# x given channel-major as well: transposes of x replaced, norm statistics by sums over partitions, first half projections on unnormalised x

## The chip, the cores and the metric

One core of one Trainium2 chip runs the kernel. The metric is the device time of one execution in microseconds (us). TensorE is called PE, its weight loads PEld, VectorE DVE, ScalarE ACT, GpSimd POOL and SyncE SP. Here SP issues every DMA; POOL and ACT issue none.

## The reference

```python
h = rmsnorm(x, norm_g)                                  # x: 1 x 2048 x 1024, float32
proj = h @ w_in                                         # 1024 -> 7680
glu_in, conv_gate, q, k, v, attn_gate, merge_logits = split(proj)
c = conformer_conv(glu_in, ...)                         # a*sigmoid(b), 31-tap depthwise conv, layernorm, silu
y_conv = (c * silu(conv_gate)) @ w_conv_out
a = sliding_window_attention(rope(q), rope(k), v, sinks)
y_attn = (a * silu(attn_gate)) @ w_attn_out
g_conv, g_attn = split(sigmoid(merge_logits))
x = x + (g_conv * y_conv + g_attn * y_attn) @ w_out
return rmsnorm(x, final_norm_g)
```

`rmsnorm(x, g)` is `x * rsqrt(mean(x*x over channels) + 1e-5) * g`, one factor for each position and one gain for each channel.

## The kernel before, in words

The 2048 positions go through in two sweeps of 1024 positions, and each sweep in two halves of 512. A projection computes 128 output channels for 512 positions (a half projection): 8 channel blocks k of 128, and for each of them three matmuls, since every float32 operand is held as a high part (rounded) and a low part (the rest): high x high, high x low, low x high. So a half projection is 24 matmuls of 128 x 128 by 128 x 512 into one bank of PSUM. Weights are split by `load_w`: SP loads a raw half (kh, four blocks k, 256 KB), ACT copies it to the high part, POOL subtracts to get the low part (lines 253 and 242), and `keep` stores the low part to DRAM, so that a second load of the same weight takes it from there. Raw, high and low tiles have four buffers each (`stage`), results three PSUM banks (`mm_ps`, tag mm) and three more for transposes, attention and the like (`tp_ps`, tag tp).

PE's right-hand operands are the tiles hT: normalised x, channels on partitions, positions along the row, high and low part, 8 tiles for each half. x comes position-major. For the first sweep `build_h_first` squares and sums each 128 positions on ACT (line 350), takes the root (351), reciprocal (353) and scales (354), and then PE transposes 128 x 128 pieces (line 361), four into one bank; ACT writes the high part times the gain (363), DVE the low part (364). The first half's transposes stand on PE ahead of the first product, the second half's among the first products. For the second sweep `build_h` does this among the output projections of the first sweep (lines 314 to 334; transposes on line 327), one block of 128 positions after another.

The first sweep begins with gb and ga (the two glu projections of channel block 0) and ka (the first of k's two). Of each the first half is computed, then of each the second half, with the weights loaded twice. Then follow kb, v, q, the other glu projections at given places, the four gates, attention and the convolution alongside, layernorm, the projections ya, yc and at last the output projection o (line 885), with the final norm.

PE's instructions run in the order in which the program writes them. On the other engines and in SP's queue a planner orders them ahead of time, by a priority (early in the program is high, evacuations of PSUM are raised by PRIO, chains of the class `Line` by twice that) and by its own estimate of when operands are ready; on the chip each engine then runs its order strictly. `Line` hangs background work (convolution taps, layernorm steps, attention chains) among PE's blocks by an estimated time.

Of the kernel before, what the change touches and what calls it, by code (L numbers as in the profile page):

```python
# [19 lines left out]
P = 128  # L20
# [33 lines left out]
def hybrid_block(ctx: ExitStack, tc: tile.TileContext, x, par_d, w_in, w_conv, sinks, w_attn, w_out,  # L54
# [47 lines left out]
    def load_first(half):  # L102
        xs = []
        for j in range(4):
            r0 = (4 * half + j) * P
            xs.append(slot(A[7 * half + j], [P, D], F32, f"xf{half}_{j}"))
            nc.sync.dma_start(out=xs[-1], in_=x2[r0:r0 + P, :])
        return xs

    x_first = load_first(0)  # L110

# [21 lines left out]
    nc.sync.dma_start(out=sink_bc, in_=sinks.partition_broadcast(P).rearrange("p o h -> p (o h)"))  # L133
    dve.tensor_scalar(out=nsink, in0=sink_bc, scalar1=-1.0, scalar2=None, op0=ALU.mult)
    par = const.tile([P, KC, NR], F32, name="par")
    nc.sync.dma_start(out=par, in_=par_d)
# [107 lines left out]
    def load_w(src, name):  # L244
# [3 lines left out]
        for kh in range(2):  # L248
            raw = stage.tile([P, 4, P], F32, tag="raw", name=f"raw_{name}{kh}")
            nc.sync.dma_start(out=raw, in_=src[:, 4 * kh:4 * kh + 4, :])  # L250
            hi = stage.tile([P, 4, P], F32R, tag="whi", name=f"whi_{name}{kh}")
            lo = stage.tile([P, 4, P], F32R, tag="wlo", name=f"wlo_{name}{kh}")
            act.copy(hi, raw)  # L253
            if (at, kh) in lo_stored:
                nc.sync.dma_start(out=f(lo), in_=d_lo[at, kh])
            else:
                split_lo(lo, raw, hi, pool)
            parts.append((hi, lo))

# [7 lines left out]
    def project(src, rhs, name, evac, halves=(0, 1)):  # L267
# [6 lines left out]
        def blocks():  # L274
            for half in halves:
                ps = mm_ps.tile([P, TH], F32, tag="mm", name=f"mm_{name}{half}")
                for k in range(KC):
                    whi, wlo = got["w"][0](k)
                    r = rhs(k, half)
                    for i, (a, b) in enumerate(((whi, r[:, 0, :]), (whi, r[:, 1, :]), (wlo, r[:, 0, :]))):  # L280
                        pe.matmul(out=ps, lhsT=a, rhs=b, start=(k == 0 and i == 0),  # L281
                                  stop=(k == KC - 1 and i == 2))
# [7 lines left out]
        def by_halves():  # L290
            return [project(src, rhs, f"{name}{h}", evac, (h,)) for h in range(2)]

        return prefetch, blocks, by_halves
# [13 lines left out]
    def build_h(s, b, tiles):  # L307

        r0 = s * T + b * P
        xt, ss = [], work.tile([P, 2], F32, tag="ss", name=f"ss{s}_{b}")  # L310
        for i in range(2):
            xh = raw_tile(f"x{s}_{b}_{i}")
            nc.sync.dma_start(out=xh, in_=x2[r0:r0 + P, i * TH:(i + 1) * TH])
            act.activation(out=t2k(f"sq{s}_{b}_{i}"), in_=xh, func=AF.Square,
                           accum_out=ss[:, i:i + 1])
            xt.append(xh)
        rs = work.tile([P, 2], F32, tag="rs", name=f"rs{s}_{b}")
        dve.tensor_tensor(out=rs[:, 0:1], in0=ss[:, 0:1], in1=ss[:, 1:2], op=ALU.add)
        act.activation(out=rs[:, 1:2], in_=rs[:, 0:1], func=AF.Sqrt, bias=eps, scale=1.0 / D)
        dve.reciprocal(out=rs[:, 0:1], in_=rs[:, 1:2])  # L320
        for i in range(2):
            dve.tensor_scalar(out=xt[i], in0=xt[i], scalar1=rs[:, 0:1], scalar2=None, op0=ALU.mult)
        yield 0.0, 8.0
        for i in range(2):
            tp = tp_ps.tile([P, 4, P], F32, tag="tp", name=f"tpx{s}_{b}_{i}")
            for j in range(4):
                pe.transpose(out=tp[:, j, :], in_=xt[i][:, j * P:(j + 1) * P], identity=ident)
            hs = t2k(f"hs{s}_{b}_{i}").rearrange("p (a b) -> p a b", b=P)
            dve.tensor_tensor(out=hs, in0=tp, in1=g_norm[:, 4 * i:4 * i + 4, :].broadcast_to([P, 4, P]),
                              op=ALU.mult)  # L330
            c0 = (b % 4) * P
            for j in range(4):
                dst = tiles[4 * i + j]
                act.copy(dst[:, 0, c0:c0 + P], hs[:, j, :])
                split_lo(dst[:, 1, c0:c0 + P], hs[:, j, :], dst[:, 0, c0:c0 + P], dve)
            yield 0.44, (1.0 if i == 0 else 0.0)
# [5 lines left out]
    ht = [make_tiles(h_tags[0], 0, "hT0_"), None]  # L342

    def build_h_first(half, xs):

        ss = work.tile([P, 2, 4], F32, tag="ss0", name=f"ssf{half}")
        for j in range(4):
            xt = xs[j]
            sq = slot(C[j], [P, D], F32, f"sqf{half}_{j}")
# [6 lines left out]
        if half == 1:  # L356
            ht[1] = make_tiles(h_tags[0], 1, "hT0_")
        for k in range(KC):
            tp = tp_ps.tile([P, 4, P], F32, tag="tp", name=f"tpf{half}_{k}")
            for j in range(4):  # L360
                pe.transpose(out=tp[:, j, :], in_=xs[j][:, k * P:(k + 1) * P], identity=ident)
# [603 lines left out]
```

## Time and profile before

| | |
|---|---|
| three runs | 2027.36, 2027.73, 2027.74 us; median 2027.73 us |
| profiled execution | 2027.62 us, of which span 2025.9 us |
| PE busy | 2004.9 us (99%) |
| DVE, ACT, POOL busy | 1324.1 (65%), 1026.0 (51%), 403.4 us (20%) |
| DMA queue | 354.16 MB, 53.9% of 16 engines |

Busy times are sums over the instructions of an engine within the span; the execution's own time holds 1.72 us that lie around the span. A group of instructions is named by its line, its engine, what it writes and reads, and its shape.

### The profile page before, as it was taken

To read this page: it belongs to the slowest core of one execution; us is meant where nothing else is said; L and a number is where in the kernel's file an instruction comes from. 1 tells how busy PE (TensorE), PEld (TensorE's weight loads), DVE (VectorE), ACT (ScalarE), POOL (GpSimd) and SP (SyncE) were. 2 spreads that over 40 slices of the span, in tenths; PEclk is the share of its full clock that TensorE was granted. 3 is DMA by queue.
4 is the path that set the end of the run, shared out by engine and by line. 5 is a ranking of instruction groups with operands and counts; after the bars stand their busy time and mean duration, and the time that the engine had idled before them with its cause. 6 is when DMAs were issued, how large, how long until landed. Compare 5 with 4: busy or idle time off the path is not lost.

```text
span 2025.9 us, 27562 instructions
## 1 busy us (share of the span) xinstructions
PE 2004.9 (99%) x9256; PEld 1666.9 (82%) x9256; DVE 1324.1 (65%) x1965; ACT 1026.0 (51%) x2313; POOL 403.4 (20%) x336
## 2 busy tenths in 40 slices
PE   7999999999999999999999999999999999999998
PEld 6888888888888888888888888888888888888887
DVE  4968779988994365123668678699888924431324
ACT  6312577767777463123533225777777764621222
POOL 2335332333323223241001120110111100001200
PEclk9999999999999999999999999999999999999999
DMA  7445655555566757445343556555555577564432
GB/s 252 146 146 167 212 172 159 161 170 180 161 189 213 245 188 249 150 151 178 134 147 132 167 181 196 159 178 177 176 157 174 175 231 260 176 229 140 152 114 83
DMA packets 265821, 355.91 MB, mean 176 GB/s; under 512 B 28112, under 2 KB 126544, under 8 KB 265680
## 3 DMA queue, kind: packets, MB, share of 16 engines
q1 hardware_dynamic: 265680, 354.16, 53.9%
q8 instruction: 73, 1.20, 0.2%
q14 instruction: 68, 0.56, 0.1%
HBM read 234.51 MB, written 119.54 MB: 175 GB/s over the span
## 4 chain that ended last, share of the span: by engine, by line
PE 94%; DVE 4%; DMA 1%; issue 0%; ACT 0%; SPq 0%; POOL 0%; DVEq 0%; ACTq 0%; POOLq 0%
PE mm_ma L281 9%; PE o L885 9%; PE mm_mc L281 9%; PE mm_yc L281 9%; PE mm_ya L281 9%; PE mm_ga L281 9%; PE mm_gb L281 8%; PE mm_cg L281 8%; PE mm_ag L281 6%; PE mm_q_a L281 4%; PE mm_q_b L281 4%; PE sc L572 3%; DVE acc L396 3%; PE ov L622 2%; PE mm_v L281 2%; PE tpp L602 1%
## 5 line engine op out<-in xcount | busy, mean ns | idle before, releaser
L396 DVE SCALAR_TENSOR_TENSOR acc<-glu,par,acc 128x1024 f32<-128x1024 f32 x464 | 595.9, 1284 | 6.2
L885 PE MATMUL o<-wo,mT 128*128 128x512 f32 x768 | 178.3, 391 | 0.0
L885 PEld LDWEIGHTS o<-wo,mT 128*128 128x128 f32 x768 | 143.1, 188 | 29.2
L281 PE MATMUL mm_cg<-hT,whi_cg 128*128 128x512 f32 x512 | 159.6, 393 | 0.0
L281 PE MATMUL mm_ma<-hT,whi_ma 128*128 128x512 f32 x512 | 159.6, 393 | 0.0
L281 PE MATMUL mm_ga<-hT,whi_ga 128*128 128x512 f32 x512 | 159.4, 392 | 0.2 <-ACT whi_ga L253 0.2
L281 PE MATMUL mm_ag<-hT,whi_ag 128*128 128x512 f32 x512 | 159.4, 392 | 0.0
L281 PE MATMUL mm_gb<-hT,whi_gb 128*128 128x512 f32 x512 | 159.2, 392 | 0.0
L281 PE MATMUL mm_mc<-hT,whi_mc 128*128 128x512 f32 x512 | 157.9, 389 | 0.0
L281 PE MATMUL mm_yc<-uT,whi_yc 128*128 128x512 f32 x512 | 157.7, 389 | 0.0
L281 PE MATMUL mm_ya<-aT,whi_ya 128*128 128x512 f32 x512 | 157.7, 389 | 0.0
L613 POOL TENSOR_SCALAR_AFFINE_SELECT pc<-pt 128x1024 fp32r<-128x1024 f32 x60 | 65.7, 1094 | 422.1 <-DVE pt L242 413.4
L281 PEld LDWEIGHTS mm_ya<-aT,whi_ya 128*128 128x128 f32 x512 | 96.1, 188 | 20.1
L281 PEld LDWEIGHTS mm_yc<-uT,whi_yc 128*128 128x128 f32 x512 | 96.1, 188 | 20.0
L281 PEld LDWEIGHTS mm_mc<-hT,whi_mc 128*128 128x128 f32 x512 | 95.9, 188 | 20.0
L281 PEld LDWEIGHTS mm_ga<-hT,whi_ga 128*128 128x128 f32 x512 | 94.4, 188 | 19.1 <-ACT whi_ga L253 0.6
L281 PEld LDWEIGHTS mm_gb<-hT,whi_gb 128*128 128x128 f32 x512 | 94.6, 188 | 18.6
L281 PEld LDWEIGHTS mm_ag<-hT,whi_ag 128*128 128x128 f32 x512 | 94.2, 188 | 18.3
L281 PEld LDWEIGHTS mm_ma<-hT,whi_ma 128*128 128x128 f32 x512 | 94.1, 188 | 18.1
L281 PEld LDWEIGHTS mm_cg<-hT,whi_cg 128*128 128x128 f32 x512 | 94.0, 188 | 18.1
L592 ACT ACTIVATE ss<-ss,st 128x128 f32<-128x128 f32 x256 | 99.7, 390 | 11.2 <-DVE st L587 10.6
L281 PE MATMUL mm_ga<-hT,wlo_ga 128*128 128x512 f32 x256 | 99.9, 390 | 0.7 <-POOL wlo_ga L242 0.7
(364 smaller groups left out, 4244.5 us busy)
## 6 DMA issues: line engine op xcount, KB each, us to landing
qk<-d_q SPq DMA_DIRECT2D x256, 64.0 KB, 2.2
d_a<-ss SPq DMA_DIRECT2D x128, 128.0 KB, 1.9
aT<-d_a SPq DMA_DIRECT2D x32, 512.0 KB, 5.7
qk<-d_k SPq DMA_DIRECT2D x240, 64.0 KB, 2.0
raw_gb<-in_w_in_dram SPq DMA_DIRECT2D x34, 256.0 KB, 3.4
raw_ga<-in_w_in_dram SPq DMA_DIRECT2D x34, 256.0 KB, 3.3
raw_ag<-in_w_in_dram SPq DMA_DIRECT2D x32, 256.0 KB, 3.6
d_ag<-ag SPq DMA_DIRECT2D x32, 256.0 KB, 2.2
```

The lines of the kernel that those rows point to most:

```text
L281: pe.matmul(out=ps, lhsT=a, rhs=b, start=(k == 0 and i == 0), stop=(k == KC - 1 and i == 2))
L396: dve.scalar_tensor_tensor(out=to, in0=glu[c][:, j:j + T], scalar=tap(c, j), in1=acc[c], op0=ALU.mult, op1=ALU.add)
L572: pe.matmul(out=o, lhsT=q[:, h, :], rhs=r, start=(j == 0), stop=(j == 1))
L592: act.activation(out=sb[:, h, :], in_=sb[:, h, :], func=AF.Exp, scale=SCALE, bias=ngm[:, h:h + 1], accum_out=den[:, h:h + 1])
L602: pe.transpose(out=tpp[:, h, :], in_=sb[:, h, :], identity=ident)
L613: pool.affine_select(out=pc, in_=f(pt), pattern=[[0, 2], [0, GQ], [1, P]], compare_op=ALU.is_ge, fill=0.0, base=0, channel_multiplier=-1)
L622: pe.matmul(out=ov, lhsT=vv, rhs=pp[:, i % 2], start=(i == 0), stop=(i == nm - 1))
L885: pe.matmul(out=ps, lhsT=a[:, c0:c0 + P], rhs=r, start=(k == 0 and i == 0), stop=(k == KC - 1 and i == 2))
```

## The change

A second copy of x, `xt`, is given channel-major (8 blocks of 128 channels by 2048 positions). All transposes of x go. Squares are summed over the 8 channel blocks elementwise (`add_square`: ACT squares, DVE or POOL adds), and the sum over the 128 partitions is two matmuls with a constant tile `ones` of 1/1024 (`norm_chain`), whose result has the mean square in every partition; ACT takes the root and DVE two reciprocals of 128 x 256, which gives `rs`, a 128 x 512 tile of factors.

In the first sweep `opening` runs six projections (gb, ga, ka, kb, q0a, q0b) for the first half on `u`, which is x times the gain, split in high and low, not normalised; their results are multiplied by `rs` when they leave PSUM (`after_rs`). The first three advance together, block k by block k, as x arrives. The second half's sum of squares is built meanwhile (adds on POOL), its `norm_chain` stands on PE after three blocks k of q0b, and then gb and ga run the second half on normalised tiles (`put_h`: DVE multiplies, ACT writes the high part, DVE the low part), then ka, kb, q0a, q0b. The normalised tiles of the first half are made among those four items. v comes after q0 instead of after k, in both sweeps. gb's and ga's weights stay in SBUF, so they are loaded once; ka, kb, q0a and q0b are loaded twice.

For the second sweep `prepare` loads x twice, once for the squares (adds on POOL) and once for the tiles.

```diff
+    def load_x(s, half, k, to):
+        nc.sync.dma_start(out=to, in_=xt[k, :, t0:t0 + TH])
+
+    def add_square(raw, total, k, name, eng):
+        if k == 0:
+            act.activation(out=total, in_=raw, func=AF.Square)
+        else:
+            sq = t2k(name)
+            act.activation(out=sq, in_=raw, func=AF.Square)
+            eng.tensor_tensor(out=total, in0=total, in1=sq, op=ALU.add)
+
+    def norm_chain(total, rs, wait, name):
+        hi, lo = (t2k(f"{name}{p}", F32R) for p in "hl")
+        act.copy(hi, total)
+        split_lo(lo, total, hi, dve)
+        yield 0.0, wait
+        ms = small_bank(f"{name}ms")
+        for i, part in enumerate((hi, lo)):
+            pe.matmul(out=ms, lhsT=ones, rhs=part, start=(i == 0), stop=(i == 1))
+        act.activation(out=rs, in_=ms, func=AF.Sqrt, bias=eps)
+        for i in range(2):
+            c = rs[:, i * (TH // 2):(i + 1) * (TH // 2)]
+            dve.reciprocal(out=c, in_=c)
+        yield 2 * MM_US, 0.0
+
+    def scaled_split(dst, src, k):
+        act.activation(out=dst[:, 0, :], in_=src, func=AF.Copy, scale=g_norm[:, k, :])
+        dve.scalar_tensor_tensor(out=dst[:, 1, :], in0=src, scalar=g_norm[:, k, :], in1=f(dst[:, 0, :]),
+                                 op0=ALU.mult, op1=ALU.subtract)
+
+    def put_h(dst, src, rs, k):
+        dve.tensor_tensor(out=src, in0=src, in1=rs, op=ALU.mult)
+        scaled_split(dst, src, k)
...
+        def first_blocks():
+            ps = [mm_ps.tile([P, TH], F32, tag="mm", name=f"mm_{p[1]}00") for p in (pa, pb, pc_)]
+            for k in range(KC):
+                scaled_split(u[k], raw[0][k], k)
+                add_square(raw[0][k], total[:, 0], k, f"sq0_{k}", dve)
+                for i in range(3):
+                    for kk in ([k] if i < 2 or k > 2 else [0, 1, 2] if k == 2 else []):
+                        product(ps[i], ws[i][0](kk), u[kk], kk)
+                        yield 3 * MM_US
+            for k in range(2):
+                ws[2][1](k)
+            with tc.high_priority(offset=2 * PRIO):
+                steps_ = list(norm_chain(total[:, 0], rs[:, 0], 0.0, "n0"))
+            yield sum(us for us, _ in steps_)
+            with tc.high_priority(offset=PRIO):
+                for p, b in zip((pa, pb, pc_), ps):
+                    after_rs(p[2])(0, b)
...
+        extra = [[lambda: load_rope(0)] + [lambda k=k: load_x(0, 1, k, raw[1][k]) for k in (0, 1)],
+                 [lambda k=k: load_x(0, 1, k, raw[1][k]) for k in (2, 3, 4, 5)],
+                 [lambda k=k: load_x(0, 1, k, raw[1][k]) for k in (6, 7)] + [lambda: load_rope(1), load_sinks]]
...
+            def with_norm(blocks=blocks, i=i):
+                for k in ((0, 1, 2), (3, 4, 5), (6, 7))[i]:
+                    add_square(raw[1][k], total[:, 1], k, f"sq1_{k}", pool)
+                for n, us in enumerate(blocks()):
+                    yield us
+                    if n == 2 and i == len(rest) - 1:
+                        with tc.high_priority(offset=2 * PRIO):
+                            steps_ = list(norm_chain(total[:, 1], rs[:, 1], 0.0, "n1"))
+                        yield sum(us for us, _ in steps_)
...
+        def both_halves_done():
+            ps = [mm_ps.tile([P, TH], F32, tag="mm", name=f"mm_{p[1]}01") for p in (pa, pb)]
             ht[1] = make_tiles(h_tags[0], 1, "hT0_")
+            for k in range(KC):
+                put_h(ht[1][k], raw[1][k], rs[:, 1], k)
+            for k in range(KC):
+                for i in range(2):
+                    product(ps[i], ws[i][0](k), ht[1][k], k)
...
+        def put_some(ks):
+            if ks[0] == 0:
+                ht[0] = make_tiles(h_tags[0], 0, "hT0_")
+            for k in ks:
+                put_h(ht[0][k], raw[0][k], rs[:, 0], k)
...
+        def prepare(n, b):
+            i = n * NB + b
+            if i < 8:
+                for k in range(2):
+                    next_square(i // 4, 2 * (i % 4) + k)
+            if i in (4, 8):
+                line.start(next_norm(i // 4 - 1))
+            if 6 <= i < 10:
+                for k in range(2):
+                    next_h(0, 2 * (i - 6) + k)
+            if i == 11:
+                ht[1] = make_tiles(h_tags[s + 1], 1, f"hT{s + 1}_")
+            if 11 <= i < 15:
+                for k in range(2):
+                    next_h(1, 2 * (i - 11) + k)
...
-                    if n == 0 and b % 2 == 1:
-                        line.start(build_h(s + 1, b // 2, ht[0]))
-                    if n == 1 and 3 <= b < 7:
-                        if b == 3:
-                            ht[1] = make_tiles(h_tags[s + 1], 1, f"hT{s + 1}_")
-                        line.start(build_h(s + 1, b + 1, ht[1]))
+                    prepare(n, b)
```

SP's order at the start of the changed kernel is par (the per-channel rows), x block 0, gb's first weight half, x 1, ga's first, x 2, ka's first, x 3, x 4, gb's second, x 5, ga's second, x 6, ka's second, x 7; then kb's two halves, the rope table of the first half and x blocks 0 and 1 of the second half; then the store of ka's low parts, q0a's weights, x blocks 2 to 5; the store of kb's low parts, q0b's weights, x blocks 6 and 7, the other rope table and the sinks.

More of the change, by code (lines that the diff above doesn't have):

```diff
@@ L99, in next_of @@
         return tags[next(rot[key])]
[L102 to L110, printed above, removed]
+    par = const.tile([P, KC, NR], F32, name="par")
+    nc.sync.dma_start(out=par, in_=par_d)
     ident_r = const.tile([P, P], F32R, name="ident_r")
@@ L256, in load_w @@
             else:
-                split_lo(lo, raw, hi, pool)
+                split_lo(lo, raw, hi, dve if steps is not None and kh == 0 else pool)
             parts.append((hi, lo))
+        for kh in range(2):
+            if steps is None:
+                part(kh)
+            else:
+                steps.append(lambda kh=kh: part(kh))
         def keep(kh):
@@ L265, in load_w, with product, small_bank, project @@
         return lambda k: (parts[k // 4][0][:, k % 4, :], parts[k // 4][1][:, k % 4, :]), keep
-    def project(src, rhs, name, evac, halves=(0, 1)):
+    def product(ps, w, r, k):
+        for i, (a, b) in enumerate(((w[0], r[:, 0, :]), (w[0], r[:, 1, :]), (w[1], r[:, 0, :]))):
+            pe.matmul(out=ps, lhsT=a, rhs=b, start=(k == 0 and i == 0), stop=(k == KC - 1 and i == 2))
+    def small_bank(name):
+        return tp_ps.tile([P, 4, P], F32, tag="tp", name=name).rearrange("p a b -> p (a b)")
+    def project(src, rhs, name, evac, halves=(0, 1), small=False):
         got = {}
@@ L275, in blocks @@
             for half in halves:
-                ps = mm_ps.tile([P, TH], F32, tag="mm", name=f"mm_{name}{half}")
+                if small:
+                    ps = small_bank(f"mm_{name}{half}")
+                else:
+                    ps = mm_ps.tile([P, TH], F32, tag="mm", name=f"mm_{name}{half}")
                 for k in range(KC):
[L278 to L282, printed above, removed]
+                    product(ps, got["w"][0](k), rhs(k, half), k)
                     if k == KC - 1:
@@ L288, in blocks @@
                     yield 3 * MM_US
-        def by_halves():
-            return [project(src, rhs, f"{name}{h}", evac, (h,)) for h in range(2)]
-        return prefetch, blocks, by_halves
+        return prefetch, blocks, (src, name, evac)
     def put_split(dst, src32, lo_eng):
@@ L380, in sweep @@
         glu, cv, acc, conv_done = {}, {}, {}, []
-        csum = work.tile([P, T], F32, tag="ln0", name=f"csum{s}", bufs=1)
+        conv_sum = []
         def conv_ops(c):
@@ L944 @@
         ("x", a["x"]),
+        ("xt", a["x"][0].T.reshape(KC, P, S)),
         ("par", rows.reshape(NR, KC, P).transpose(2, 1, 0)),
```

186 lines of the change are left out of this document (106 added, 80 removed).

## The prediction

> **What bounds the kernel now.** I read the page's head first, then who waited for whom on PE, then the chain that ended last, then tables by stage for its places without products.
>
> ```profile
> span 2025.9 us, 27562 instructions
> PE 2004.9 (99%) x9256; PEld 1666.9 (82%) x9256; DVE 1324.1 (65%) x1965; ACT 1026.0 (51%) x2313; POOL 403.4 (20%) x336
> PE tpf L361 <- DVE ident_r L117: 8.4, 1, 8.4
> PE tpf L361 <- DVE xf L354: 2.3, 2, 1.4
> PE sc L572 <- DVE pt L242: 1.3, 1, 1.3
> 0.00:40.26 40.26, 27.74 (x136) 21.90 (x137) 20.96 (x40) 28.82 (x53) 9.10 (x16) 1.00 0.77 277
> 930.74:1036.31 105.57, 105.57 (x498) 87.31 (x497) 61.82 (x163) 50.77 (x163) 2.67 (x4) 1.00 0.45 159
> 1931.85:2018.90 87.05, 87.04 (x384) 71.72 (x383) 28.51 (x47) 19.85 (x48) 1.29 (x1) 1.00 0.21 83
> 18.63 0.70 PE L281 MATMUL mm_gb<-hT,whi_gb 128*128 128x512 f32 x2
> 40.26 0.62 PE L281 MATMUL mm_gb<-hT,whi_gb 128*128 128x512 f32 x2
> 1931.85 87.05 PE o L885 x384
> 930.74 19.05 PE o L885 x84
> 1036.31 10.88 PE mm_ga L281 x48
> ```
>
> PE is the bound: 21.0 us of the span have no PE work, and 12.52 of them lie ahead of 40.26 (40.26 less 27.74). The last output stage is 384 products in 87.05 us, so a product costs 0.2267 us. So the path can shorten in two places only. (a) The opening: gb, ga and ka of the first half, 72 products or 16.32 us, are through at 40.26, so 23.94 us of the opening hold no product: 18.63 before the first one and the rest the second half's transposes and small waits. (b) The seam: from the first output product (930.74) to ga's first of the second sweep (1036.31) lie 384 + 48 products, 97.93 us, in 105.57. The 64 transposes cost 7.64. After 40.26 PE waits 1.3 us for `sc`; the rest of its idle time is the tail, which the change leaves alone.
>
> **The change, part by part.** These are the prices.
>
> ```profile
> GB/s 0 0 0 0 61 225 348 410 379 430 348 410 266 297 358 358 399 369 301 147 95 86 105 221 350 343 369 389 405 410 405 399 405 430 430 415 410 410 420 410
> 4.36 1.06 ACT L350 ACTIVATE sqf<-xf 128x1024 f32<-128x1024 f32 x1 [2.06 <-DMA xf<-in_x_dram]
> L253 ACT CAST whi_gb<-raw_gb 128x512 fp32r<-128x512 f32 x34 | 20.8, 619 | 18.0 <-PE mm_q_a L281 9.5 <-PE tpx L327 3.0 <-PE mm_ag L281 2.3
> L314 ACT ACTIVATE sq<-x 128x512 f32<-128x512 f32 x16 | 9.8, 616 | 0.0
> L708 ACT ACTIVATE rstd<-lnvar,eps_t 128x512 f32<-128x512 f32 x4 | 2.5, 684 | 0.0
> L684 DVE RECIPROCAL rstd<-rstd 128x256 f32<-128x256 f32 x8 | 13.2, 1710 | 31.4 <-ACT rstd L708 31.4
> L364 DVE SCALAR_TENSOR_TENSOR hT<-tpf,par,hT 128x512 fp32r<-128x512 f32 x16 | 11.9, 751 | 11.7 <-ACT hT L363 11.5
> L469 DVE TENSOR_TENSOR rb_k<-mm_kb,cs 128x512 f32<-128x512 f32 x4 | 2.7, 684 | 0.1
> L242 POOL TENSOR_TENSOR wlo_gb<-raw_gb,whi_gb 128x512 fp32r<-128x512 f32 x16 | 20.7, 1297 | 64.2 <-ACT whi_gb L253 62.7 <-DMA d_cg<-cg 1.5
> 64.51 1.30 POOL L472 TENSOR_TENSOR ra_k<-ra_k,rb_k 128x512 f32<-128x512 f32 x1
> 65.24 2.81 DVE L242 TENSOR_TENSOR hl_k<-ra_k,hl_k 128x512 fp32r<-128x512 f32 x2 [0.26 <-ACT hl_k L296]
> 65.86 1.64 POOL L242 TENSOR_TENSOR wlo_v<-raw_v,whi_v 128x512 fp32r<-128x512 f32 x1
> L361 PE MATMUL tpf<-ident_r,xf 128*128 128x128 f32 x24 | 6.0, 430 | 10.7 <-DVE ident_r L117 8.4 <-DVE xf L354 2.3
> L361 PE MATMUL tpf<-ident_r,xf 128*128 128x128 f32 x32 | 4.8, 272 | 0.0
> ```
>
> **Seam.** The transposes go: -7.64. Two `norm_chain`s add four products: +0.91. The rest lies beside PE: 16 extra x loads (DMA share 0.45 there); on DVE 16 times 0.684 + 0.751 and four reciprocals, 29.8 us, for what before were 64 small splits, 16 multiplies and scalings; on POOL 14 adds of 1.30 where it worked 2.67 of 105.57. Two blocks k are squared in each 5.44-us block, and the sum has another block and 6 us before PE asks. Should cover fail, the wait is one chain of about 3 us for each half (bounds 0 to 6); I take 0. Sum -6.73.
>
> **Start.** PE waits for x block 0 and gb's first half, 256 KB each behind par's 140. In the bandwidth row (slices of 0.4 us) these 0.67 MB have moved by 3.7 us; the first 512 KB of x were used at 4.36, about 1 us after they had moved. So gb's weights are there at 4.8, then ACT 0.62 and waiting beside a square 0.62: first product at 6.0 (bounds 5.5 and 8.4, where `ident_r` came late on DVE by its place in the order). No transposes have run by then. The first 24 transposes, between 8.4 and 16.5 us, took 430 ns each (first of the two L361 rows), those between 26 and 40 us 272, while the stage's granted clock is 1.00: PE is slow at first. If half pace lasts some 4 us of dense products, it costs 2.2 (bounds 0, since no row shows a product in that state, and 4 if it lasts 8.1 us as it did for the transposes; I take the middle). Small waits between blocks k: 0.3. ACT's 22 operations (16 on x, 6 casts, 13.6 us) and DVE's 18 keep ahead of 16.32 us of products, and 3.8 MB at 400 GB/s are in by about 13. Products of the first three end at 6.0 + 2.2 + 0.3 + 16.32 = 24.8.
>
> By the Trainium skill (TensorE: Matmul & The Clock Gate, Part 1) PE starts at half clock until about 3.4 us of sustained work. The two L361 rows agree in kind. As an estimate from that page the sum would have 1.7 here for my 2.2.
>
> **First norm.** Two products, 0.45; the sum of squares is ready before them (0, bound 2). Its two reciprocals hold DVE 3.42 and put off evacuations, but kb and q0a go to other banks: hidden. Then 57 products (kb, q0a, three blocks of q0b), 12.92: PE asks for the second norm at 38.2.
>
> **Second norm, the change's new wait.** On POOL must be done by then: 3 + 6 weight splits, 7 adds, and 2 of k's rope, 18 x 1.30 = 23.4 us, from about 10 us on; q0b's splits can't begin before kb's buffers come free (26 and 29). POOL alone would make it. But DVE and POOL get in each other's way when both read two SBUF operands: at 64.51 to 67.5 the two DVE subtractions took 2.81 where 0.68 is usual, each lasting until a POOL operation ended, and POOL's took 1.64. In the new opening nearly all DVE work is such (raw x and its high part, squares, and factors from `t2k` instead of PSUM). Some 12 operations of 0.62 between 10 and 38 go in POOL's way, 7 us: 30 us for 28. I take 1.5 of waiting (bounds 0 and 6); behind it on PE stands everything. With 0.45 for the two products the norm is out at M = 40.2.
>
> **Gap after it.** PE has 15 products of q0b left, to M + 3.4. The tiles need the root 0.68, two reciprocals 3.42, then DVE multiply 0.68, ACT 0.62, DVE low part 0.75, with 0.6 of signals: M + 6.8. q0b's evacuation (three DVE operations, 1.9) has priority and comes between: M + 8.0 for the high parts with the low ones just behind. So PE waits 4.6 (bounds 2.8 without the evacuation, 7). Then gb and ga want two tile parts a block, DVE 1.43, PE 1.36: DVE paces, and k's and q's low parts and POOL's rope add: 1.6 more (bounds 0 and 5). Both are through at M + 3.4 + 4.6 + 10.88 + 1.6 = 60.7. That is 192 products, 43.52 us, so the opening now loses 17.2.
>
> **After.** For the first half's tiles DVE does 8 x 1.43 beside convolution and rope within 21.8 us, before v needs them: 0.5 (bounds 0 and 3). ka, kb, q0a and q0b find weights loaded a second time, the low parts from DRAM: hidden, PE needs a weight each 5.44 us. v's later place: 0.
>
> Sum: opening -23.94 + 17.2 = -6.7; after it +0.5; seam -6.7: -12.9. The profiled execution took 2027.62 (span 2025.9 and 1.72 around it), 0.11 under the median shown. 2027.62 - 12.9 + 0.11 = **2014.8**.
>
> **Rivals.** *Better covered:* the second norm doesn't wait, evacuation comes behind the tiles, DVE keeps pace: the opening loses 6.0 + 2.2 + 0.9 + 2.8 = 11.9 and nothing follows: -12.0 - 6.7 gives 2009.0. For it: POOL was busy 9.10 of 40.26, DVE 20.96. Against: L684's 1710 ns, twice, in the gap.
>
> *DVE and POOL bind:* every one of the 18 POOL operations makes a DVE operation wait and the other way round. First norm 2 late, second 6, pace 5, v 3: 16, 12.4 more than my 3.6. A late first norm takes 2 off the second's wait, and that wait gives POOL time for what would slow the pace, 4: 6.4 more, 2021.2. For it the 2.81-us row; against, POOL's operations come spread, as weights land.
>
> The Trainium skill (SBUF — State Buffer, Who interferes with whom) says that the two share an interface under an exclusive lock, held for the instruction. The 2.81-us row agrees; fully held, this rival is what it gives.
>
> *Slower, by SP's queue:* the stores of ka's and kb's low parts stand ahead of x blocks 2 to 7 of the second half and wait for POOL.
>
> ```profile
> SPq L263 <- POOL wlo_ga L242: 8.5, 2, 5.7
> ```
>
> Each us that x block 7 lands after about 33 goes to PE, since the second norm stands in its order. At 400 GB/s the 9 MB up to it land at about 27, so 6 us are free; 13 more make the change worthless. A landing at 48 would give 2030 or so. Against: the longest such wait was 5.7, and by the prices above POOL is through kb's at about 20 (an estimate).
>
> **How the numbers follow.** No change is within 0.2%, 4.1 us. Likeliest case 0.55 (2011 to 2018), better covered 0.20 (2006.5 to 2011), DVE and POOL 0.17 (2018 to 2023), SP's queue 0.08, of which 0.03 within 0.2% and 0.05 slower. With a sliver of the third case within 0.2%: faster 0.91, same 0.04, slower 0.05. The range 2006.5 to 2021.5 leaves out the last and the ends of its neighbours, under 2 in 10.
>
> **What would show it.** Right: no transposes of x; first product near 6 us and slow for some 4; one PE wait behind the second norm of about 1.5 and a larger one, 4 to 5, for the first normalised tile; the output stage at 87 plus 0.9. Wrong: products of the first three strung out by x or ACT; the second norm late by 5 or more with POOL full; PE waiting in the seam; or v waiting for tiles.

## The result, and the profile after

The changed kernel takes 2059.24 us (median of four runs, 2058.82 to 2059.73) where before takes 2027.55: 31.7 us more, a ratio of 1.0157 with a 95% interval of 1.0139 to 1.0174. The prediction was 2014.8, and its range ended at 2021.5. PE is still what the end hangs on. The head of the page after, and who waited for whom on PE (us in total, times, longest):

```profile
span 2057.4 us, 27299 instructions
PE 2001.0 (97%) x9136; PEld 1660.0 (81%) x9136; DVE 1356.2 (66%) x1921; ACT 1025.7 (50%) x2249; POOL 439.1 (21%) x354
PE mm_ya L271 <- DVE mp L906: 20.3, 1, 20.3
PE n1ms L332 <- ACT n1h L327: 12.9, 1, 12.9
PE mm_gb L271 <- ACT w L249: 7.9, 1, 7.9
PE mm_gb L271 <- ACT hT L340: 4.2, 2, 2.8
PE mm_gb L271 <- DVE hT L341: 1.9, 2, 1.6
PE o L1025 <- DVE wo L234: 1.0, 1, 1.0
```

The 7.9 is the start, ahead of the first product. Two other waits are long. The 12.9 belongs to the change: the second norm's products (`n1ms`) wait for the high copy of the sum of squares. The longest, 20.3, is in a stage that the change doesn't touch, the projection ya in the middle of the first sweep. A table by stage of the kernel after (length, then busy time of PE, PEld, DVE, ACT, POOL, then granted clock, DMA share, GB/s):

```profile
0.00:40.26 40.26, 32.37 (x131) 25.64 (x131) 30.68 (x37) 24.81 (x42) 19.09 (x20) 1.00 0.80 271
40.26:81.05 40.79, 21.75 (x67) 15.67 (x66) 35.05 (x43) 15.75 (x24) 14.47 (x11) 0.71 0.45 149
770.31:880.13 109.82, 89.52 (x386) 73.66 (x385) 39.65 (x55) 30.68 (x43) 28.02 (x16) 0.91 0.49 165
967.17:1067.65 100.48, 99.45 (x437) 81.70 (x437) 60.84 (x89) 45.52 (x94) 21.06 (x18) 1.00 0.59 205
```

At 81.05 gb and ga of the second half are through; by then PE has done 192 products (43.5 us), so the opening loses 37.5 us where before it lost 23.9: +13.6. ya's 384 products (87.05 us at full pace) take 109.82: +22.8. The seam, 105.57 before, takes 100.48: -5.1. That sums to +31.3; the spans differ by 31.5. So one third of the loss is the opening, two thirds are ya, and the seam gives a gain of about the size that was expected. In both bad stages the granted clock is below 1.

### The profile page after: what moved, and what is told of

Same layout as the page of the kernel before. It is cut to its first block, busy times and chain, and to the rows that moved or that the text cites. A ratio compares the mean times of both kernels' runs of the same rounds, so it can differ in the third digit from the quotient of the medians.

```text
span 2057.4 us, 27299 instructions
## 1 busy us (share of the span) xinstructions
PE 2001.0 (97%) x9136; PEld 1660.0 (81%) x9136; DVE 1356.2 (66%) x1921; ACT 1025.7 (50%) x2249; POOL 439.1 (21%) x354
## 4 chain that ended last, share of the span: by engine, by line
PE 59%; DVE 1%; DMA 1%; issue 0%; ACT 0%; DVEq 0%; SPq 0%; ACTq 0%
PE mm_yc L271 8%; PE mm_ya L271 8%; PE o L1025 7%; PE mm_ma L271 4%; PE mm_cg L271 4%; PE mm_ag L271 4%; PE mm_gb L271 4%; PE mm_ga L271 4%; PE mm_mc L271 4%; PE mm_q_b L271 2%; PE mm_q_a L271 2%; PE sc L683 1%; PE ov L733 1%; PE mm_v L271 1%; PE tpp L713 1%; PE mm_ka L271 1%
## 5 line engine op out<-in xcount | busy, mean ns | idle before, releaser
L271 PE MATMUL mm_ya<-aT,whi_ya 128*128 128x512 f32 x512 | 159.4, 393 | 20.3 <-DVE mp L906 20.3
L1025 PEld LDWEIGHTS o<-wo,mT 128*128 128x128 f32 x768 | 144.1, 188 | 31.3 <-DVE wo L234 1.4
L271 PE MATMUL mm_gb<-hT,whi_gb 128*128 128x512 f32 x480 | 149.5, 393 | 0.0
L271 PE MATMUL mm_ga<-hT,whi_ga 128*128 128x512 f32 x480 | 149.1, 392 | 0.0
L271 PEld LDWEIGHTS mm_ga<-hT,whi_ga 128*128 128x128 f32 x480 | 88.8, 188 | 17.6
L271 PEld LDWEIGHTS mm_gb<-hT,whi_gb 128*128 128x128 f32 x480 | 88.5, 188 | 17.5
L271 PE MATMUL mm_ya<-aT,wlo_ya 128*128 128x512 f32 x256 | 100.3, 392 | 0.0
```

What stands on the lines that cost most here:

```text
L1025: pe.matmul(out=ps, lhsT=a[:, c0:c0 + P], rhs=r, start=(k == 0 and i == 0), stop=(k == KC - 1 and i == 2))
```

## Why ya waits: an order written out by hand

DVE in the first 40 us of ya, from the timeline of the kernel after (start, duration):

```profile
763.24 6.59 DVE L795 RECIPROCAL rstd<-rstd 128x256 f32<-128x256 f32 x4 [14.15 <-ACT rstd L819]
769.86 9.13 DVE L798 TENSOR_TENSOR cv<-cv,rstd 128x1024 f32<-128x1024 f32 x7
797.06 0.69 DVE L830 TENSOR_TENSOR lcg<-lcg,cv 128x512 f32<-128x512 f32 x1 [6.69 <-DMA lcg<-d_cg]
806.34 0.69 DVE L906 TENSOR_TENSOR mp<-mm_ya,lma 128x512 f32<-128x512 f32 x1 [0.30 <-DMA lma<-d_ma]
```

`mp` is the evacuation of ya. Until it comes, ya's results hold their PSUM banks, and PE stops once these are full. In the kernel before, the first `mp` began at 763.1, 6.6 us into ya; here at 806.3, 36 us into it. In between DVE does the end of the layernorm of the first sweep's convolution: its reciprocals start 7 us ahead of ya (in before 19.5 us ahead), and the steps that make `uT`, the layernorm's result, all stand in front of `mp`. In before these steps (765 to 792 us) stand among ya's evacuations. The reason is in ya's evacuation:

```python
if half == 0:
    if ("u", e, 1) not in stored:
        line.finish()
```

If the background steps that make u(e) aren't written out yet when ya's evacuation is, all that are left are written ahead of it. `Line` hands them out by a time of its own, which starts when the first convolution is queued. That happens in the evacuation of ga's second half, and this now stands behind four more half projections: at 44.6 of the program's own time instead of 30.1, worked out by following how the program writes its order. By the same time of the program ya came no later (731.8, before 734.4). So the convolution and all behind it lost 14.5 us of cover, u(0) wasn't written out yet, and the remaining steps went ahead of `mp`. This is read from the program; two experiments test it.

**e1: the background's clock set back by the 14.5 us.**

```diff
+                    if s == 0 and c == 0:
+                        line.bg_t = line.t - 14.5
                     line.bg.extend(conv_ops(c))
```

> The changed kernel, with the background clock of the Line class set back by 14.5 us when the first convolution is queued; nothing else. Theory A (order): the 20.3-us wait of PE in ya comes from program order. The first convolution is queued at line time 44.6 instead of 30.1, so layernorm's steps are still in the background queue when ya's first result is evacuated, line.finish() writes all of them ahead of the evacuation, and the evacuation stands behind them on every engine. With the clock set back they are through in time: the wait is gone, the slow products behind it too, 2036 us (2034 to 2039). Theory B (lateness): the opening ends some 13 us later on the chip, so that DVE and ACT reach layernorm late whatever the program's order: the wait stays at 15 or more, 2053 to 2060 us.

Measured: 2037.94 us (2037.75 to 2039.12), ratio to before 1.0053 (1.004 to 1.0067), 21.3 less than the changed kernel. ya's 384 products, by the table of this kernel:

```profile
771.50:858.40 86.90, 86.90 (x385) 71.97 (x384) 34.56 (x47) 26.70 (x40) 24.08 (x17) 1.00 0.61 200
```

Full pace, no wait. The opening is as it was (PE waits 12.9 for the second norm, and ga is through at 80.25). The `uT` steps on DVE run when they did, from 781.3 to 806.9 (changed kernel: 781.3 to 807.0); only the first `mp`, at 777.2, no longer stands behind them. That is order and not lateness.

**e2: the kernel before, with that clock put forward by 14.5 (`line.bg_t = line.t + 14.5`), and nothing else.**

> The kernel before, with the background clock set forward by 14.5 us when the first convolution is queued; nothing else is changed, the transposes are all there. Theory A: the order of layernorm and of ya's first evacuation tips as in the changed kernel, PE waits some 20 us in ya for mp and runs slowly behind it: 2047 to 2052 us. Theory B: the opening is not late here, so nothing happens: 2026 to 2030 us.

Measured: 2049.63 us (2048.93 to 2051.34), ratio 1.0111 (1.0097 to 1.0125), 22.5 us slower than before, with the same wait in the list of PE's waits:

```profile
PE mm_ya L281 <- DVE mp L801: 19.4, 1, 19.4
```

So this cause is shown from both sides: with the change and without it, 14.5 us of lag in the background's clock cost 21 to 23 us. Neither operation nor transfer was added there; only the order moved.

## The seam alone

**e3: the kernel before, with the second sweep's `prepare` and loads of the changed kernel, and the first sweep as before.**

> The kernel before with only the second sweep's tiles made the new way (x channel-major, squares added on POOL, sum over partitions by two products, no transposes there); the opening is the old one. From the changed kernel's trace: its stretch from the first output product to ga is 100.48 us against 105.57, so 2022.5 us (2021.5 to 2023.5). The prediction's term of 6.7 would give 2020.8. If DVE's added work or the doubled loads of x make PE wait elsewhere, 2025 or more.

Measured: 2021.94 us (2021.54 to 2022.5), ratio 0.9973 (0.9963 to 0.9984), 5.2 us faster. The stage from the first output product to ga:

```profile
930.90:1031.40 100.50, 99.40 (x437) 81.61 (x437) 60.90 (x89) 45.60 (x94) 21.17 (x18) 1.00 0.60 204
```

432 products are 97.93 and the four of the norms 0.91; 1.1 us of this stage has no work on PE. 1.0 of it is a new wait of the output products for the low part of their weights (`o <- wo`, as in the list above). The norms themselves are covered. What makes `wo` late is not shown: DVE is no busier in this stage than before (60.90 against 61.82), but its order there is another, and POOL is (21.17 against 2.67).

## What the opening loses

PE and, below it, the engines that it waits for, from the timeline of the kernel after:

```profile
7.89 1.65 PE L271 MATMUL mm_gb<-u,w 128*128 128x512 f32 x3 [7.89 <-ACT w L249]
13.25 0.84 PE L271 MATMUL mm_gb<-u,w 128*128 128x512 f32 x3
53.33 0.79 PE L332 MATMUL n1ms<-n1h,ones 128*128 128x512 f32 x1 [12.91 <-ACT n1h L327]
62.24 0.51 PE L271 MATMUL mm_gb<-hT,w 128*128 128x512 f32 x1 [2.82 <-ACT hT L340]
72.92 1.44 PE L271 MATMUL mm_ga<-hT,w 128*128 128x512 f32 x3
74.20 0.85 PE L271 MATMUL mm_gb<-hT,w 128*128 128x512 f32 x3
6.08 0.72 ACT L340 ACTIVATE u<-xr,par 128x512 fp32r<-128x512 f32 x1 [3.79 <-DMA xr<-in_xt_dram]
44.56 0.62 ACT L301 CAST hl_k<-ra_k 128x512 fp32r<-128x512 f32 x1 [5.26 <-POOL ra_k L582]
47.90 0.62 ACT L301 CAST hl_k<-ra_k 128x512 fp32r<-128x512 f32 x1 [2.72 <-POOL ra_k L583]
48.42 1.15 ACT L321 ACTIVATE sq<-xr_x 128x512 f32<-128x512 f32 x2
49.19 3.44 POOL L322 TENSOR_TENSOR total<-total,sq 128x512 f32<-128x512 f32 x2 [1.32 <-ACT sq L321]
52.66 0.62 ACT L327 CAST n1h<-total 128x512 fp32r<-128x512 f32 x1 [2.59 <-POOL total L322]
```

Read ACT's lines from 44.56 on: it stands idle 5.26 us in front of k's first high cast, which waits for a rotary sum of POOL, then 2.72 in front of the second. The last two squares of the second half come only behind these, at 48.42; then POOL's adds, then the copy `n1h`, then PE. ACT isn't full (15.75 us busy of 40.79); it is held in its fixed order by an operation that another engine makes late. POOL, which makes it, was busy 16.77 of the 18.96 us between 33.67 and 52.63. The rest of the section asks what in this chain matters.

**e4: e1, with the squares of the second half in buffers of their own** instead of the five `t2k` buffers, which they shared with the unnormalised results.

```diff
-                    add_square(raw[1][k], total[:, 1], k, f"sq1_{k}", pool)
+                    add_square(raw[1][k], total[:, 1], k, f"sq1_{k}", pool, H[8 + k])
```

> The changed kernel with the clock set back as in e1, and the squares of the second half written to eight tiles of their own (the slots that its normalised tiles take later) instead of the five shared buffers t2k. Theory C (buffers): the five buffers are held by the first norm's two parts and the three un-normalised results, so squares 1 and later wait until the first norm is out and are put behind the weight casts on ACT; with tiles of their own the second norm's sum is ready when PE asks: PE's wait of 12.9 us falls to 3 or less, products stay fast, gb and ga of the second half end near 65 us instead of 81, and the time falls 13 to 17 under e1, to 2019 to 2023. Theory D (shared reads of DVE and POOL): each add on POOL takes 1.7 instead of 1.3 and each DVE operation beside it 1.75 instead of 0.68; that stays, the wait stays at 8 or more, 2030 or more.

Measured: 2031.05 us (2030.15 to 2032.72), ratio 1.002 (1.0011 to 1.0029), 6.9 less than e1. The wait fell from 12.9 to 7.4: between the two expectations. Timeline of e4:

```profile
39.13 1.70 POOL L322 TENSOR_TENSOR total<-total,sq 128x512 f32<-128x512 f32 x1
42.54 0.62 ACT L301 CAST hl_k<-ra_k 128x512 fp32r<-128x512 f32 x1 [8.01 <-POOL ra_k L584]
44.28 0.62 ACT L301 CAST hl_k<-ra_k 128x512 fp32r<-128x512 f32 x1 [1.13 <-POOL ra_k L585]
45.95 0.60 ACT L327 CAST n1h<-total 128x512 fp32r<-128x512 f32 x1
```

The squares now run early and the sum is complete at 40.83, about when PE asks for it (39.2). The copy still runs 5.1 us later, behind k's casts. So the buffers were 5.5 us of the wait. Most of what is left of the wait is spent in ACT's list; whether that list also sets the end of the opening is taken up behind e10.

**e5: e1, with 54 filler products in PE's 12.9-us wait.**

```diff
+        for _ in range(n_fill):
+            pe.matmul(out=ms, lhsT=fill[0], rhs=fill[1], start=True, stop=True)
```

> The kernel of e1 (changed kernel, background clock set back) with 54 filler products on PE just ahead of the second norm's two products: 12.2 us of full-speed work in the place of the 12.9 us in which PE waited; their sums are overwritten. They do no work of the reference. Everything else is as in e1, where PE asked for the second norm at about 40, was through with gb and ga of the second half at 80.25, and the time was 2037.94. Theory (PE loses pace by standing still, and that costs time after the wait): the rest of q_b no longer takes 4.7 us but 3.4, gb's and ga's groups of three products take 0.7 us each from the start where they took 1.3 up to 73, and the two are through 2 to 3 us earlier, at 77 to 78.5; the time is 2035 to 2036. Rival (the normalised tiles, made by DVE, set the pace alone): the products are faster one by one, but the two are through less than 1 us earlier and the time stays within 1 of 2037.9.

Measured: 2041.92 us (2040.56 to 2042.65), ratio 1.0069 (1.0054 to 1.0084), 4.0 slower than e1; both expectations missed. The part on the pace held: the rest of q_b's products took 3.6 us instead of 4.7. But the planner, which counts the fillers, now thought the norm late and put three high parts of the first half's tiles ahead of its root on ACT (timeline of e5):

```profile
55.98 1.34 ACT L342 ACTIVATE hT<-xr,par 128x512 fp32r<-128x512 f32 x2 [1.75 <-DVE xr L347]
58.63 0.69 ACT L335 ACTIVATE rs<-n1ms,eps_t 128x512 f32<-128x512 f32 x1
```

In e1 the root ran at 54.17. As a test of the pace this kernel is spoilt (e10 repeats it without moving the order); as a test of the order it says that a worse place in ACT's list (the root 4.5 us later) put off ga's end by 3.0 us, from 80.25 to 83.22.

**e6: e4, with the seven adds on DVE instead of POOL** (`f"sq1_{k}", dve, H[8 + k]`).

> The kernel of e4 (clock set back, the second half's squares in buffers of their own) with the seven adds of the second half's squares moved from POOL to DVE. e4: wait for the second norm 7.4, time 2031.05. Theory (DVE and POOL hold each other up, and that is what makes the sum and k's rope late): POOL has 7 x 1.72 = 12 us less to do between 25 and 41, DVE's two-operand work goes back from 1.75 to about 0.7 for much of that stretch, and the wait falls to 2 to 5; the time is 2026 to 2029. Rival (the place of the high copy in ACT's order, behind the casts of k's rope, sets it): the wait stays at 6 or more, and the time within 2 of 2031.

Measured: 2032.43 us (2030.94 to 2034.47), ratio 1.0025 (1.0016 to 1.0035): as e4 within its scatter, wait 6.9. The contention did go: k's rotary products on DVE take 0.68 where they took 1.75 in e4, and ACT casts k at 39.49 instead of 42.54. Yet the last add, now in DVE's list behind k's low parts and q's evacuation, came at 44.90 (timeline of e6):

```profile
37.03 0.68 DVE L582 TENSOR_TENSOR rb_k<-un,cs 128x512 f32<-128x512 f32 x1
44.90 0.68 DVE L322 TENSOR_TENSOR total<-total,sq 128x512 f32<-128x512 f32 x1
45.67 0.62 ACT L327 CAST n1h<-total 128x512 fp32r<-128x512 f32 x1 [2.78 <-DVE total L322]
```

So DVE and POOL holding each other up is real: without it k's casts came 3 us earlier. But the seven adds in DVE's own list used up what that gained, so e6 shows only that moving the adds doesn't pay; it does not show how much of e4's wait the contention is.

**e7: e4, with q1a and q1b also run on unnormalised x ahead of the second norm** (10.9 us more of real work; v behind them; the clock set back by 25.4 in all). **e8: e7, with the norm's copy queued after the squares, its products at the end of q1a, and the tiles made beside q1b.**

> The kernel of e4 with two more half projections (q1a and q1b of the first half, 48 products, 10.9 us of real work) run on unnormalised x ahead of the second norm, and v behind them; the background clock is set back by as much more (25.4 in all). Theory (the second norm is late against PE, by a time that does not grow with the work put in front): PE reaches the norm 10.9 us later and waits 0 to 2 there instead of 7.4, without losing pace; the gap of the tiles behind it (12 in e4) stays at 8 to 12. Time 2020 to 2025. Rival (ACT, DVE and POOL are full in the opening, so that more work in front puts the norm off too): the wait stays at 5 or more, and the time at 2028 or above.

> The kernel of e7 with the steps of the second norm in other places: its high copy and low part as soon as the squares are summed, its two products at the end of q1a, and the second half's normalised tiles made beside q1b's products, ahead of gb and ga that need them. Theory (tiles can be made beside products, so that the gap goes): no wait at the norm above 1, the wait for the first tiles falls from 8 to 12 to 2 to 5; the opening loses some 16 us where the kernel before loses 23.9, and with the seam's 5.2 the time is 2013 to 2018. Rival (DVE is the bound of the opening, so that the order of its work matters little): the time stays within 2 of e7's.

Measured: e7 2035.07 us (2034.31 to 2036.88), ratio 1.0038 (1.0023 to 1.0053); e8 2035.66 (2033.79 to 2036.01), ratio 1.0038 (1.0023 to 1.0052). Both are some 4 us slower than e4. Both theories fell, and the numbers of both rivals came: e7's wait is above 5 and its time above 2028, e8's time within 2 of e7's. In e7 PE asks for the norm at 56.6 instead of 39.2 (10.9 us of products, 2.7 of new waits for q1a's weights, and slow products behind these) and still waits 6.4, since the copy moved too; it now stands behind q's casts as well (timeline of e7, then PE's waits of e8):

```profile
60.66 0.62 ACT L301 CAST hl_q__0_1_504<-ra_q__0_444 128x512 fp32r<-128x512 f32 x1 [0.61 <-POOL ra_q__0_444 L586]
62.33 0.60 ACT L327 CAST n1h<-total 128x512 fp32r<-128x512 f32 x1
```

```profile
PE mm_gb L271 <- ACT hT L340: 7.4, 2, 6.8
PE n1ms L332 <- ACT n1h L327: 3.1, 1, 3.1
```

e8 shortens the wait at the norm to 3.1 and gets a wait of 6.8 for the first tile in exchange. Each projection on unnormalised x brings PE 5.4 us of cover, and ACT, DVE and POOL the rescaling and, for k and q, the rotary work, in front of the norm.

**e9: e4 without most of the rotary work of k and q_0 in the first half** (six of eight products and the four sums are left out).

> The kernel of e4 (background clock set back, the second half's squares in buffers of their own; wait for the second norm 7.4, which ends at 46.6) without most of the rotary embedding of k and q_0 for the first half of the first sweep: of its eight products with the cos and sin tables two are kept, and the four sums on POOL are left out; the casts and low parts of k and q take the unrotated values. The work left out is 6 DVE operations and 4 POOL operations, of which 3 and 2 lie before the norm. Theory (the norm's copy stands in ACT's fixed order behind k's casts, and these wait for the rope sums that POOL makes last): ACT no longer waits 8 us for POOL there, and the norm's products start at 39 to 42, a wait of 0 to 3. Rival (the sum of squares itself is late, since POOL is full and DVE holds it up): the sum ends at 39 or later as before, and the wait stays at 4 or more.

Measured: 2024.65 us (2022.87 to 2028.23), ratio 0.9988 (0.9978 to 0.9998), with less to compute than the others. The wait falls to 3.9 (0.5 more for the low part), between theory and rival again, while ga ends at 66.0 instead of 73.1 and the time falls by 6.4: more than the wait gives (timeline of e9):

```profile
39.03 1.71 POOL L322 TENSOR_TENSOR total<-total,sq 128x512 f32<-128x512 f32 x1
41.40 0.72 ACT L340 ACTIVATE hT<-xr,par 128x512 fp32r<-128x512 f32 x1 [5.16 <-DVE xr L345]
42.54 0.61 ACT L327 CAST n1h<-total 128x512 fp32r<-128x512 f32 x1
```

The sum is there at 40.74, 1.5 after PE asks: that is POOL's share. The other 1.8 is again ACT's list: ahead of the copy stands a tile of the *first* half, which nobody needs yet and which waits for DVE. Why the planner put it there is not shown.

**e10: e4, with 26 fillers in the waits for the first two tiles behind the norm** (2.20, 1.62 and 1.28 us), 10 ahead of gb's first product, 8 behind it, 8 ahead of the next tile's. Up to there ACT, DVE and POOL keep e4's order.

> The kernel of e4 with 26 filler products in PE's waits for the first two normalised tiles of the second half: 10 ahead of gb's first product, 8 between it and the second, 8 ahead of the second tile's; they go to a bank that nothing reads. ACT, DVE and POOL keep their order up to there. In e4 the first of these products was at 55.72, the last of ga at 73.1, and gb's and ga's groups of three took 1.3 us each until 65.6 and 0.69 from there. Theory (PE loses pace by standing still, and this puts off the end): the groups take 0.69 from the first tile on, PE then waits for tiles only, the last of which is there at 69.6 in e4, and both are through at 70.5 to 71.2; the time falls by 1.9 to 2.6, to 2028.5 to 2029.2. Rival (the tiles set the pace alone, the slow products being hidden in the waits): through at 72.6 or later, and the time within 0.6 of 2031.

Measured: 2028.79 us (2027.97 to 2031.24), ratio 1.0007 (0.9998 to 1.0016), 2.3 less than e4: a time as the theory had it, though the end of ga moved by only 1.6 (73.1 to 71.5, expected 70.5 to 71.2). The two intervals overlap (e4's begins at 1.0011); the two profiled executions are 1.9 apart (2030.65 and 2028.76), 1.6 of it by the end of ga. The timelines of e4 and of e10, the group of three products of the first tile and the first product behind ga:

```profile
58.42 1.19 PE L271 MATMUL mm_ga<-hT,w 128*128 128x512 f32 x3
73.12 0.61 PE L271 MATMUL mm_ka<-hT,whi_ka 128*128 128x512 f32 x2
```

```profile
58.46 0.86 PE L460 MATMUL mm_ga<-hT,w 128*128 128x512 f32 x3
71.49 0.61 PE L271 MATMUL mm_ka<-hT,whi_ka 128*128 128x512 f32 x2
```

Useless work made the kernel about 2 us faster, because PE kept its pace. This is the one place where the lost pace is priced by itself.

**What these runs leave open: DVE's load.** The account so far follows PE's wait back through ACT's list. DVE gives another reading, which is e8's rival. The engines' busy times between 28 and 70 us (columns as in the tables above), in e4 and, for comparison, in e12 of the next section, in which PE doesn't wait in this stretch; and the last low part of e4's second half:

```profile
28.00:70.00 42.00, 29.00 (x102) 21.41 (x101) 41.57 (x48) 19.13 (x29) 20.18 (x15) 0.80 0.60 204
28.00:70.00 42.00, 42.00 (x185) 34.29 (x184) 34.13 (x41) 20.43 (x32) 16.05 (x14) 1.00 0.75 245
68.85 0.74 DVE L341 SCALAR_TENSOR_TENSOR hT<-xr_x,par,hT 128x512 fp32r<-128x512 f32 x1
```

In e4 DVE is busy 41.57 of these 42.00 us, in the changed kernel 39.30, in before 25.36. Here it counts as busy also while POOL holds it up. In e4 it has made the last tile at 69.6, with hardly an idle moment before, and PE is through with ga 3.5 us later. So an earlier copy on ACT alone would move PE's wait, but not this last tile: for that DVE must have less to do, or do first what PE waits for (up to there it also does four multiplies and two low parts of the first half's tiles, and q's rotary work). e9 fits this too: it takes work off DVE, and its last tile is there at 64.5. How the opening's remaining loss splits between DVE's load and the order of the lists, no run separates.

## A version that beats both

The runs don't speak against the sum over partitions itself. What stands out in the opening is that PE has only unnormalised work in front of the second norm, and that this work loads the engines and the lists in which the norm stands.

**e11 and e12: e3, with the first half of the first sweep as before (transposed, normalised), and only the second half of x channel-major.** Its squares are added on DVE, its norm stands near the end of ga, its tiles are made while PE works on the first half: five projections in e11, four in e12, where before has three.

```diff
+    def second_half():
+        for k in range(KC):
+            add_square(raw_x[k], total, k, f"sq0_{k}", dve, sq[k // 2][:, k % 2])
+        yield 0.0, 7.0
+        yield from norm_chain(total, rs, 2.5, "n1")
+        ht[1] = make_tiles(h_tags[0], 1, "hT0_")
+        for k in range(KC):
+            put_h(ht[1][k], raw_x[k], rs, k)
...
-            line.start(build_h_first(1, xs))
+            line.start(second_half())
```

> The kernel of e3 (before, with the change in the second sweep alone; 2021.94) with a smaller change in the first sweep too: the first half keeps its transposes and is normalised before any product; only the second half of x comes channel-major, its 32 transposes go, its squares are summed on DVE ahead of everything else that DVE does for the blocks, and its norm stands near the end of ga. Five projections (gb, ga, ka, kb, v's first) run on the first half before the second half's tiles are needed, instead of three; the background clock is set back by 11.4, so that the steps come in the order of before. Nothing runs on unnormalised x, so the rotary work starts when PE has five blocks in front of it. Theory (the changed opening loses because the second norm has too little normalised work in front of it, and its few operations stand behind rotary work): no PE wait over 1 at the second norm or at the first tiles of the second half; the ten blocks, 240 products or 54.4 us, are through at 71.5 to 73.5, so that the opening loses 17 to 19 where before loses 23.9; the time is 2015 to 2018. Rival (any norm by sums in the opening puts some PE wait of several us in the transposes' place): a wait of 3 or more, and a time of 2020 or above.

> The kernel of e11 with four projections (gb, ga, ka, kb) on the first half instead of five, and the clock set back by 5.5. Theory: PE asks for the second half's first tile at about 40 instead of 45.5; the tiles, which DVE ends every 1.43 us from about 34 on, are then needed every 0.68, and PE waits 1 to 4 for them; the time is 1 to 4 above that of e11. Rival (the tiles are early enough for both): within 1 of e11.

Measured: e11 2019.58 us (2019.15 to 2020.59), ratio 0.9963 (0.9949 to 0.9977); e12 2018.18 (2017.75 to 2020.02), ratio 0.9957 (0.9945 to 0.997). e12 is 8.9 us faster than before and 3.8 faster than the seam alone. By its table it has no idle PE between 40 and 80 us:

```profile
40.00:60.00 20.00, 20.00 (x88) 16.08 (x87) 16.61 (x23) 9.98 (x16) 5.34 (x5) 1.00 0.80 257
60.00:80.00 20.00, 20.00 (x92) 16.56 (x91) 18.37 (x19) 6.57 (x13) 7.67 (x6) 1.00 0.53 184
```

Its eight blocks, 192 products, are through at 63.0: the opening loses 19.5. The theory's main point held in both, no wait at the norm or for a tile of the second half. Its size missed: e11's ten blocks are through at 75.9 (expected 71.5 to 73.5), a loss of 21.5, and its time is 1.6 above the expected range; e12, expected 1 to 4 above e11, is 1.4 below, with intervals that overlap. These kernels differ from the changed one in several things at once (nothing to rescale, adds on DVE, more normalised work in front, less load on DVE), so they show that the smaller change pays, and not which of these it owes that to. e11 has one wait that e12 hasn't, for a PSUM bank that k's evacuation frees late on DVE:

```profile
PE mm_gb L281 <- DVE ra_k L488: 1.4, 1, 1.4
```

## The prediction, step by step

Two steps failed: that nothing behind 40.26 outside the seam would change (put at 0 but for 0.5 at v; ya alone cost 22.8), and the second norm with what follows it (1.5 of waiting predicted, 12.9 measured, and 5.9 more up to the end of ga).

- **The bound and the two places.** Right as a reading of before. The sentence "After 40.26 PE waits 1.3 us for `sc`; the rest of its idle time is the tail, which the change leaves alone" is the step that failed most: 22.8 of the 44.4 us between 2014.8 and 2059.24 arose in ya, at a wait that before doesn't have. The prediction priced each moved step's DMAs and queues, but not the background steps, whose clock starts with the moved one (e1, e2).
- **Seam, -6.7.** -5.1 in the changed kernel, -5.2 alone. The cover held for the norms (taken at 0, bound 6); the 1.6 missing are 1.0 for `wo` and smaller gaps.
- **Start: first product at 6.0, bounds 5.5 to 8.4.** 7.89: x's first block was used at 6.08, where 4.8 was taken for the operands, and a square's first value and the weight's cast stood behind it. **Slow PE 2.2 and small waits 0.3:** 2.6 together; the first 12 products took until 13.25, 5.36 us instead of 2.72. The weight loads among them waited 1.3 us in sum for casts and low parts, so not all of this is slow pace. From 13.25 to PE's asking for the second norm, 40.4, products run without a gap; 38.2 was predicted, and the difference is the start. The hidden reciprocals and the first norm were right.
- **Second norm, 1.5, bounds 0 and 6.** 12.9. The estimate was made from POOL's load, and POOL's sum alone would have come to about that (in e4 and e9 it is complete 1.5 to 1.7 us after PE asks). What was left out: the five `t2k` buffers (5.5 by e4) and ACT's fixed order, in which squares and copy stand behind casts that wait for POOL (most of the rest, by e4 and e9). For this wait the prediction added up what POOL has to do and didn't write down in which order each engine would do its part; that DVE would be busy nearly all the time (39.30 of 42.00 us from 28 to 70) it did not see.
- **The gap, 4.6, and DVE's pace, 1.6.** From the norm's end to the end of ga, 20.5 predicted, 26.4 measured (54.65 to 81.05). The waits for tiles are 6.1 together, near the 6.2 of the two terms; that is partly luck, since slower products between the waits shorten them. What was left out is PE's pace, which the prediction charged only at the start: behind the 12.9 the rest of q0b took 1.4 longer than at full pace, and gb and ga, slow until 74.2, some 4.6 longer. In e4's kernel e10 recovers 1.6 of this.
- **v, 0.5.** No wait for v shows.
- **Rivals.** Better covered: no. DVE and POOL bind: its second norm 6 late is half of the 12.9 that came, and e4 puts 5.5 of these down to buffers that it didn't name. Whether it is right about the rest is open: DVE was nearly full and POOL's operations did slow it, and e6, which took the contention away, gave DVE seven more operations. SP's queue: no square of the last four x blocks waited for its load; their only idle time in front is 1.6 us for DVE, by the groups of the kernel after between 20 and 82 us:

```profile
L321 ACT ACTIVATE sq<-xr_x 128x512 f32<-128x512 f32 x4 | 2.3, 622 | 1.6 <-DVE glu L534 1.6
```

- **Signs named ahead.** "The second norm late by 5 or more with POOL full" came true: late by 12.9, with POOL busy 16.77 of 18.96 us while the sum was made (33.67 to 52.63).

Two things stay open. With the clock mended and buffers of their own, the opening loses 29.6 us instead of 37.5, and the 17.2 predicted were never reached; no run put the norm's few operations first in every engine's list or took the first half's tiles out of DVE's, so whether the idea as such can gain is not shown. And all runs with the changed opening and the clock set back have a new wait of 1.5 to 2.0 us behind the gate mc, whose cause wasn't looked into.

## What to carry to other kernels

Where engines run lists that were ordered ahead of time, a moved step takes with it everything that is counted from it: before pricing the move, follow what else starts by the same event, also hundreds of us later. A short operation that PE waits for is as late as the slowest thing ahead of it in its engine's list, and more cover in front doesn't help if the cover itself fills those lists. Look also at which engine is full in the stage in question, and not over the whole kernel: DVE is busy 66% of the span here, and nearly all of the opening. Try the parts of a change apart: here one part was worth 5.2 us, half of another 3.8, and the whole cost 31.7.

## What the runs showed of the hardware that was not expected

- PE loses its pace by short waits. In e4 waits of 2.20 and 1.62 us with a single product between them were followed, from about 58.5 on, by products of 0.43 us until about 65.5, with further waits of 1.28 and 0.32 among them; with fillers in the first three (e10) they took 0.23. In e7 waits of 1.17 and 1.54 with two products between did the same; in e9 waits of 2.80 and 0.61 did not. The Trainium skill (TensorE: Matmul & The Clock Gate, Part 1) puts the return to half clock behind an idle window of about 3.4 us; the waits of e4 and e7 are each shorter, and those of e7 even together, so the trace doesn't agree with that as a rule on the length of a wait.
- The granted clock shows it in part only: 0.71 for 40.26 to 81.05, but 1.00 for the first 40.26 us, in which the first 12 products took 0.45 us each (part of that may be waiting for weights).
- A DVE operation on two SBUF operands took 1.75 instead of 0.68 beside POOL's adds and weight splits, four of them in a row in e4 (34.54 to 41.31), and 0.68 in e6, where POOL stood idle beside them. The Trainium skill (SBUF — State Buffer, Who interferes with whom) has the two engines lock each other out for a whole instruction; the trace agrees in kind, with 1.07 us for each such meeting.
